# A two-layer encoder trunk on one core: issuing the first weight block, the x blocks and the leading pair's last steps when their engines can begin them, and interleaving the first loads

## The chip, the cores and the metric

The kernel runs on one NeuronCore of a Trainium2 chip. Its engines are TensorE (PE, matrix products into PSUM), VectorE (DVE), ScalarE (ACT), GpSimd (POOL, which here only issues DMAs) and SyncE (SP, which issues DMAs too). Each engine works through its own queue in the order in which the program was written, and waits at an instruction until the semaphores that it names have arrived. The metric is the device time of one execution, in microseconds (us). Before the change it is 1428.33 us, the median of 3 runs (1427.67 to 1429.08).

## The reference

Two layers (`DEPTH = 2`) over 512 tokens of width 1024, all in float32. Cut to what matters here:

```python
for l in range(DEPTH):
    h = rms_norm(x, attn_norm_g[l])
    z = jnp.einsum('bsd,dc->bsc', h, w_in[l])
    qa, ka, va, qb, kb, vb, ga, gb = jnp.split(z, IN_SPLITS, axis=-1)
    ...
    ya = jnp.einsum('bsc,cd->bsd', window_gqa(qa, ka, va, sink_a[l]), w_proj_a[l])
    ...
    yb = jnp.einsum('bsc,cd->bsd', neighbourhood_attn(qb, kb, vb, rel_bias_b[l]), w_proj_b[l])
    mixed = jax.nn.sigmoid(ga) * ya + jax.nn.sigmoid(gb) * yb
    x = x + jnp.einsum('bsd,de->bse', mixed, w_out[l])
    h = rms_norm(x, ffn_norm_g[l])
    u = jax.nn.silu(jnp.einsum('bsd,df->bsf', h, w_gate[l])) * jnp.einsum('bsd,df->bsf', h, w_up[l])
    x = x + jnp.einsum('bsf,fd->bsd', u, w_down[l])
```

`w_in` is 1024 x 4352, the feed-forward width is 2816.

## The kernel before, in words

**Split operands.** Every float32 operand of a product is cut into a high part (a cast to the type that TensorE multiplies, F32R) and a low part (operand minus high part), and a product is three matmuls: high x high, high x low, low x high. A high part is a cast on ACT (`A.copy`), a low part a subtraction on DVE. Where it can be done early, a weight's low part is made by a DMA instead: ACT writes the negated high part, and a DMA of POOL's queue adds the weights to it (`w_low`, `low_by_transfer`).

**The order is written by a planner.** `trunk` runs twice. The first, dry pass keeps a modelled clock per engine (`clock`, `ready`, `cost`) and decides with it when each step is written into the program; the second pass repeats the decisions and emits the instructions. Steps off the main line are generators, called chains: a chain yields a `Need` (tiles that must be ready on an engine, PSUM slots, keys of other steps, and how far that engine's modelled clock may run ahead, `backlog`), and `drive` writes a chain's next step as soon as its `Need` is met at the modelled time of TensorE. A string that the main line yields is a key that must be done before the main line goes on (`force`). Other steps are not asked: `at_pos(t, f)` and `soon(f)` write f at a fixed place in TensorE's modelled order. From the dry pass come also the lifetimes of the SBUF buffers, and `Layout.pack` places them in two arenas (names `arena_72`, float32, and `arena_73`, F32R), so a write can have to wait for the last reader of what lay there before.

**The start.** `x_load(c)` fetches the eight 128-column blocks of x on SP's queue. `first_load(i)` fetches the first projection's weights in four slabs of 512 KB: slab 0 in two halves on ACT's queue, slabs 1 to 3 on POOL's. POOL's queue also carries the small vectors: `consts` (328 KB), the b-branch norm gains (into `vec2`), `positions`, the a-branch norm gains (`gqa`) and the sinks (`snk`). `start(nrm, k)` then prepares block k for the first `token_matmul`: TensorE turns the x block (4 transposes), ACT and DVE make the high and low parts of the weights (`first_parts`) and of x times the norm's gain, and ACT squares. `chain_tables` puts on DVE, among these, the steps of the rotary tables, the first of which read `posi` and `snk`.

**The feed-forward part of a layer.** 2816 hidden columns are one leading pair of 128-column tiles and five quads of 512 columns (`QUADS = 5`). The leading pair is computed in plain form: 48 matmuls of 512 columns for gate, 48 for up (`pair_matmul`), with `evac_g` and `evac_u` taking the results out of PSUM. Each quad is computed by seven block products of a Strassen scheme (`ORDER = (1, 5, 6, 2, 7, 3, 4)`, `m_step`), for gate and then for up: 24 matmuls of 256 columns each. Product m needs the parts of a weight combination (class `Quad`: `high(m)`, `low(m)`) and of an x combination (`chain_x`: blocks b11, b12, b21, b22 of the normalised x, with sums `n1`, `n2`). Products 1, 5 and 2 accumulate in banks of the pool `at`; product 6 goes into a bank of the pool `mm` that ACT first fills with the result of product 1 (`seed`), so product 6 cannot begin before that copy. `seed_c` (DVE) then makes the bank of product 3 out of product 6's. Between the products stand the down-projection steps `("d", ...)`, 6 or 12 matmuls each; the first eight use the leading pair's hidden tiles (`u[0]`, `u[1]`), which `evac_u` multiplies and splits.

**What sets the order around the change.** In each layer the first quad of gate has its steps moved ahead by up to 18 us of modelled time (`early` in `plan_ffn`), `Quad.due` writes `high(m)` 6.5 us before the product's modelled time and `low(m)` 1.8 us later, whatever the engines are doing. `chain_x` writes the cast of a block right behind the instruction that makes it, and `evac_u` writes its five instructions at one go where the pair's last matmul is written.

All instructions are recorded in one helper, so that the profile shows line L309 for nearly all of them; they are told apart by engine, operation and tile. `mm` and `at` are PSUM banks.

## Time and profile before

| | before |
|---|---|
| median of 3 runs | 1428.33 us (1427.67 to 1429.08) |
| profiled execution | 1429.13 us, of which the profile's span is 1426.4 us |
| PE busy | 1393.8 us (98%), 8074 matmuls and transposes |
| DVE, ACT, POOL busy | 935.4, 713.0 and 317.7 us |
| DMA | 208.49 MB, mean 146 GB/s |
| chain that ended last | PE 85%, DVE 10%, ACT 2%, DMA 1% |

Busy time counts from an instruction's start to its end, and neighbours overlap: eight DVE subtractions of 1.22 us that start every 1.14 us keep it busy without a gap. "[5.29 <-ACT mm L309]" behind a row is idle time of that engine just before it, and what ended it.

### The profile page before, as it was taken

What the parts mean: (1) busy time and instruction counts of PE and PEld (TensorE: products, weight loads), DVE (VectorE), ACT (ScalarE), POOL (GpSimd) and SP (SyncE); (2) the same over time, 40 slices, a digit from 0 to 9 for tenths busy, and PEclk for the clock granted to TensorE, in tenths of its full rate; (3) what the DMA queues carried; (4) which work ended last, traced back from release to release, by engine and by line L of the source; (5) the groups of instructions that cost most, each with busy time, mean ns of one, the idle gap of its engine ahead of it and who ended that gap; (6) DMA issues with size and microseconds to landing.
All of it is one profiled execution on the core that took longest, in us unless ns stands there. A gap on an engine that the chain in (4) does not pass through costs nothing.

```text
span 1426.4 us, 20963 instructions
## 1 busy us (share of the span) xinstructions
PE 1393.8 (98%) x8074; PEld 1223.7 (86%) x8074; DVE 935.4 (66%) x1768; ACT 713.0 (50%) x1209; POOL 317.7 (22%) x325
## 2 busy tenths in 40 slices
PE   7999999999989999999999999999998999999998
PEld 5788888888889999999987888888887999999997
DVE  5877788455867566575648869774567657575753
ACT  6476766543653343343545776674445433343441
POOL 4443222310121111101353332223012120111110
PEclk9999999999999999999999999999999999999999
DMA  8877988885486565736798678979557484745545
GB/s 203 171 135 133 165 156 148 158 196 147 91 183 141 119 149 131 180 77 131 148 188 180 125 138 154 172 137 204 146 137 132 121 194 102 177 100 138 129 93 118
DMA packets 197299, 208.49 MB, mean 146 GB/s; under 512 B 25532, under 2 KB 167024, under 8 KB 197200
## 3 DMA queue, kind: packets, MB, share of 16 engines
q0 software_dynamic: 134944, 141.53, 53.6%
q1 hardware_dynamic: 61904, 65.09, 15.7%
q8 instruction: 63, 1.03, 0.3%
q10 hardware_dynamic: 352, 0.54, 0.1%
q14 instruction: 36, 0.29, 0.1%
HBM read 194.55 MB, written 2.10 MB: 138 GB/s over the span
## 4 chain that ended last, share of the span: by engine, by line
PE 85%; DVE 10%; ACT 2%; DMA 1%; issue 1%; POOL 0%; DVEq 0%; ACTq 0%; POOLq 0%
PE mm L309 65%; PE at L309 20%; DVE arena L309 7%; DVE sm L309 3%; ACT arena L309 2%; DMA cst<-in_consts 1%; DMA snk<-in_sink_a 0%; DMA arena<-in_w_in 0%; POOL arena L309 0%; ACT L309 0%; DVE hf L309 0%; ACT mm L309 0%; DVE den L309 0%; ACT sm L309 0%; DVEq L1619 0%
## 5 line engine op out<-in xcount | busy, mean ns | idle before, releaser
L309 PE MATMUL mm<-arena 128*128 128x512 f32 (+1 forms) x5568 | 1126.6, 357 | 15.2 <-ACT mm L309 10.6
L309 PEld LDWEIGHTS mm<-arena 128*128 128x128 f32 x5568 | 906.6, 191 | 147.7 <-ACT mm L309 11.0
L309 ACT CAST arena<-arena 128x1024 fp32r<-128x1024 f32 (+2 forms) x278 | 236.0, 870 | 235.9 <-DVE arena L309 232.6
L309 PE MATMUL at<-arena 128*128 128x256 f32 (+2 forms) x1952 | 301.5, 295 | 1.8 <-DVE arena L309 1.6
L309 DVE TENSOR_TENSOR arena<-arena,arena 128x1024 fp32r<-128x1024 f32 (+2 forms) x268 | 262.2, 993 | 55.5 <-ACT arena L309 55.2
L309 PEld LDWEIGHTS at<-arena 128*128 128x128 f32 x1952 | 265.3, 191 | 20.8 <-DVE arena L309 5.0
L309 ACT ACTIVATE arena<-arena 128x1024 fp32r<-128x1024 f32 (+3 forms) x252 | 207.6, 843 | 122.4 <-DMA arena<-in_w_down 59.0
L309 DVE TENSOR_TENSOR arena<-arena,mm 128x512 f32<-128x512 f32 x144 | 98.9, 687 | 233.3 <-PE mm L309 233.2
L309 POOL DMA_DIRECT2D arena<-in_w_in x163 | 163.1, 1397 | 335.4 <-ACT arena L309 330.6
L309 POOL DMA_DIRECT2D arena<-in_w_down x96 | 99.4, 1233 | 502.4 <-ACT arena L309 316.8
L309 DVE TENSOR_TENSOR arena<-arena 128x1024 f32<-128x1024 f32 (+4 forms) x196 | 158.5, 823 | 2.5
L309 DVE TENSOR_TENSOR arena<-at,arena 128x384 fp32r<-128x384 f32 (+4 forms) x206 | 114.8, 562 | 63.0 <-ACT arena L309 55.5
L309 ACT CAST arena<-at 128x384 fp32r<-128x384 f32 (+2 forms) x164 | 74.6, 458 | 106.9 <-PE at L309 93.0
L309 PE MATMUL at<-cst,arena 128*128 128x128 f32 x504 | 85.7, 276 | 5.2 <-DVE arena L309 4.3
L309 PEld LDWEIGHTS at<-cst,arena 128*128 128x128 f32 x504 | 64.0, 141 | 22.5 <-DVE arena L309 5.8
L309 ACT ACTIVATE arena<-arena,negm 128x256 f32<-128x256 f32 (+1 forms) x128 | 71.5, 560 | 16.8 <-DVE negm L309 16.0
L309 ACT COPY arena<-at 128x512 f32<-128x512 f32 (+1 forms) x68 | 39.5, 582 | 64.0 <-PE at L309 63.6
L309 DVE TENSOR_TENSOR arena<-mm,arena 128x512 f32<-128x512 f32 x72 | 49.3, 687 | 27.2 <-PE mm L309 26.8
L309 DVE CUSTOM_DVE_ANT_0 arena<-at,cst,nsnk 128x256 f32<-128x256 f32 (+1 forms) x64 | 34.5, 546 | 20.0 <-PE at L309 19.8
L309 ACT ACTIVATE arena<-arena,vecT 128x512 fp32r<-128x512 f32 x24 | 17.4, 726 | 54.4 <-DVE arena L309 53.9
L309 DVE CUSTOM_DVE_ANT_0 arena<-at,arena 128x256 f32<-128x256 f32 (+1 forms) x64 | 30.7, 486 | 8.9 <-PE at L309 8.4
L309 POOL DMA_DIRECT2D arena<-in_w_up x8 | 8.2, 1029 | 125.3 <-PE mm L309 77.7
(69 smaller groups left out, 429.7 us busy)
## 6 DMA issues: line engine op xcount, KB each, us to landing
arena<-in_w_in POOLq DMA_DIRECT2D x99, 512.0 KB, 7.2
arena<-in_w_down POOLq DMA_DIRECT2D x80, 512.0 KB, 6.8
arena<-in_w_gate SPq DMA_DIRECT2D x20, 1024.0 KB, 7.2
arena<-in_w_up SPq DMA_DIRECT2D x20, 1024.0 KB, 5.1
arena<-in_w_in POOLq DMA_DIRECT2D x64, 256.0 KB, 6.2
arena<-in_w_proj_a POOLq DMA_DIRECT2D x16, 512.0 KB, 7.2
arena<-in_w_proj_b POOLq DMA_DIRECT2D x16, 512.0 KB, 7.3
arena<-in_w_out SPq DMA_DIRECT2D x16, 512.0 KB, 6.1
```

The lines of the kernel that those rows point to most:

```text
L309: f(*args, **kw)
```

## The change

First quad of gate (class `Quad`, `first`): its steps are no longer written at fixed positions but by a chain, which waits for each product's due position, then writes the sums on DVE, waits until the source is ready for ACT before it writes the cast, and until the cast is ready for DVE before it writes the low part. `chain_x`: every cast now waits in the planner for its source. The leading pair's last steps: `evac_u` only takes the result out of PSUM, and a chain per tile writes the product with the gate, the cast and the low part when their sources are ready; the main line waits for them (keys `u0`, `u1`) before the first down-projection step. The planner's model counts a bank that a matmul adds to as a source. At the start, POOL's queue takes small loads and slabs in turns, and for block 0 the transposes and the cast of x are written ahead of the weights' parts.

```diff
-                start = max([clock[self.key]] + [at_(name_of(x), self.key) for x in aps[1:]])
+                sources = aps if kw.get("start") is False else aps[1:]
+                start = max([clock[self.key]] + [at_(name_of(x), self.key) for x in sources])
...
     def drive(main):
         for u in main:
-            if isinstance(u, str):
+            if isinstance(u, (str, tuple)):
                 force(lambda: u in done)
...
             (self.a11, self.a21), (self.a12, self.a22) = ((t[:, :, :256], t[:, :, 256:]) for t in self.raw)
+            self.s1 = buf([4, 256])
+            if self.first:
+                spawn(self.chain())
 
         def due(self, m, t):
-            at_pos(t - LEAD_PREP, lambda: self.high(m))
+            if self.first:
+                at_pos(t - LEAD_PREP, lambda: done.add((self, m)))
+                return
+            at_pos(t - LEAD_PREP, lambda: (self.sums(m), self.high(m)))
             at_pos(t - LEAD_PREP + 1.8, lambda: self.low(m))
 
-        def high(self, m):
+        def chain(self):
+
+
+            for m in ORDER:
+                yield Need(keys=[(self, m)], backlog=XLOG)
+                self.sums(m)
+                yield Need("act", [self.source(m)])
+                self.high(m)
+                yield Need("dve", [self.parts[m][1]], backlog=XLOG)
+                self.low(m)
+                done.add((self, m, "parts"))
...
+    first_load(0)
     for c in range(KD):
         x_load(c)
-        if c % 2 == 0:
-            first_load(c // 2)
-    GQ.dma_start(cst[:, P:], a["consts"][:, P:])
-    for i, n in enumerate(("q_norm_b", "k_norm_b")):
-        for h in range(2):
-            GQ.dma_start(vec2[2 * i : 2 * i + 2, HD * h : HD * h + HD], a[n])
     posi = cp.tile([P, P], I32, tag="posi", name="posi")
...
+    for i, n in enumerate(("q_norm_b", "k_norm_b")):
+        for h in range(2):
+            GQ.dma_start(vec2[2 * i : 2 * i + 2, HD * h : HD * h + HD], a[n])
+    first_load(1)
     gqa = cp.tile([P, 2, DEPTH, HD], F32, tag="gqa", name="gqa")
...
+    first_load(2)
+    GQ.dma_start(cst[:, P:], a["consts"][:, P:])
+    first_load(3)
...
-        first_parts(k)
         ps = at_bank()
         for b in range(NB):
             T.transpose(ps[:, P * b : P * b + P], xin[k][:, b, :], ident)
+        if k:
+            first_parts(k)
         A.activation(held(nrm.xh[k]), by_columns(ps), AF.Copy, scale=gain(0, k))
+        if not k:
+            first_parts(k)
...
             def high(m, src):
+                yield Need("act", [src], backlog=XLOG)
                 h = buf([4, 256], F32R)
                 A.copy(h, src)
...
-            high(6, n2)
+            yield from high(6, n2)
...
             V.tensor_tensor(t, ps, nrm.rows, ALU.mult)
+            u.append((act(F32R), act(F32R)))
+            spawn(chain_u(j, t))
+
+        def chain_u(j, t):
+            yield Need("dve", [t, gt[j]])
             V.tensor_tensor(gt[j], t, gt[j], ALU.mult)
-            h, lo = act(F32R), act(F32R)
-            split(gt[j], h, lo)
-            u.append((h, lo))
+            yield Need("act", [gt[j]])
+            yield from gsplit(gt[j], *u[j])
+            done.add(f"{key}u{j}")
...
                 yield f"x{l}{m}"
+                if quads[l, q, w].first:
+                    yield (quads[l, q, w], m, "parts")
                 yield from m_step(q, w, m)
...
+                if f0 == 0:
+                    yield f"{key}u0"
+                    yield f"{key}u1"
```

The order of the matmuls on PE and of the loads on SP stays. Three places where the order moves:

ACT, first layer, from the last parts of the quad's weights to the seed of product 6. `CAST ... 128x1024` is a high part of a weight or x block, `ACTIVATE arena_73<-arena_73 128x1024` the negated copy for a low part by transfer, `ACTIVATE arena_72<-arena_72 128x512` the silu of a gate tile, `CAST ... 128x512` the high part of a hidden tile, `COPY mm<-at` the seed. Before:

```order
L309 CAST arena_73<-arena_72 128x1024 x4
L309 ACTIVATE arena_72<-arena_72 128x512 x2
L309 CAST arena_73<-arena_72 128x1024
L309 ACTIVATE arena_73<-arena_73 128x1024
L309 CAST arena_73<-arena_72 128x1024 x3
L309 CAST arena_73<-arena_72 128x512
L309 ACTIVATE arena_73<-arena_73 128x1024
L309 CAST arena_73<-arena_72 128x512
L309 CAST arena_73<-arena_72 128x1024
L309 COPY mm_3506<-at_3474 128x512
```

The same stretch of ACT after the change, to the hidden tiles' casts:

```order
L309 ACTIVATE arena_72<-arena_72 128x512 x2
L309 CAST arena_73<-arena_72 128x1024 x2
L309 ACTIVATE arena_73<-arena_73 128x1024
L309 CAST arena_73<-arena_72 128x1024 x4
L309 ACTIVATE arena_73<-arena_73 128x1024
L309 CAST arena_73<-arena_72 128x1024
L309 ACTIVATE arena_73<-arena_73 128x1024
L309 COPY mm_3501<-at_3464 128x512
L309 CAST arena_73<-arena_72 128x1024
L309 ACTIVATE arena_73<-arena_73 128x512
L309 CAST arena_73<-arena_72 128x1024
L309 COPY arena_72<-at_3497 128x512
L309 CAST arena_73<-arena_72 128x512 x2
```

The two casts of the hidden tiles stood ahead of the seed and now stand behind it; the negated copies of products 3 and 4 now both stand ahead of it.

DVE at the same place, from the copy of the row scales on. `128x1024` rows into arena_73 are low parts, `SCALAR_TENSOR_TENSOR ... vecT 128x512 x4` normalises half of x, `mm_3290`, `mm_3291` are the pair's gate banks, `mm_3401`, `mm_3402` (after the change `mm_3392`, `mm_3393`) its up banks, `mm_3506` (`mm_3501`) the bank of product 6. Before, from the second half of x:

```order
L309 SCALAR_TENSOR_TENSOR arena_72<-arena_72 128x1024
L309 TENSOR_TENSOR arena_72<-mm_3290,arena_72 128x512
L309 TENSOR_TENSOR arena_72<-mm_3291,arena_72 128x512
L309 TENSOR_TENSOR arena_73<-arena_72,arena_73 128x1024 x3
L309 TENSOR_TENSOR arena_72<-arena_72 128x4x256
L309 TENSOR_TENSOR arena_73<-arena_72,arena_73 128x1024
L309 TENSOR_TENSOR arena_72<-arena_72 128x4x256
L309 TENSOR_TENSOR arena_72<-mm_3401,arena_72 128x512
L309 TENSOR_TENSOR arena_72<-arena_72 128x512
L309 TENSOR_TENSOR arena_73<-arena_72,arena_73 128x512
L309 TENSOR_TENSOR arena_72<-mm_3402,arena_72 128x512
L309 TENSOR_TENSOR arena_72<-arena_72 128x512
```

After:

```order
L309 TENSOR_TENSOR arena_73<-arena_72,arena_73 128x1024
L309 SCALAR_TENSOR_TENSOR arena_72<-arena_72,vecT 128x512 x4
L309 SCALAR_TENSOR_TENSOR arena_72<-arena_72 128x1024
L309 TENSOR_TENSOR arena_72<-arena_72 128x4x256
L309 TENSOR_TENSOR arena_72<-mm_3392,arena_72 128x512
L309 TENSOR_TENSOR arena_73<-arena_72,arena_73 128x1024 x3
L309 TENSOR_TENSOR arena_72<-arena_72 128x4x256
L309 TENSOR_TENSOR arena_72<-mm_3393,arena_72 128x512
L309 TENSOR_TENSOR arena_72<-arena_72 128x512
L309 TENSOR_TENSOR arena_73<-arena_72,arena_73 128x1024
L309 TENSOR_TENSOR arena_72<-arena_72 128x512
L309 TENSOR_TENSOR arena_73<-arena_72,arena_73 128x1024
```

The gate evacuations moved ahead of the second half of x, together with one low part, the first up evacuation moved ahead of three low parts, and the low parts of the hidden tiles left this stretch.

POOL's queue at the start. `arena_72<-in_w_in 128x2x512` is a slab of 512 KB:

```order
-L309 DMA arena_72<-in_w_in 128x2x512 x3
-L309 DMA cst<-in_consts 128x656
+L309 DMA posi<-in_positions 4x8x16
 L309 DMA vec_76<-in_q_norm_b 2x64 x2
 L309 DMA vec_76<-in_k_norm_b 2x64 x2
-L309 DMA posi<-in_positions 4x8x16
+L309 DMA arena_72<-in_w_in 128x2x512
 L309 DMA gqa<-in_q_norm_a 128x128
 L309 DMA gqa<-in_k_norm_a 128x128
+L309 DMA arena_72<-in_w_in 128x2x512
+L309 DMA cst<-in_consts 128x656
+L309 DMA arena_72<-in_w_in 128x2x512
 L309 DMA snk<-in_sink_a 128x16
```

The three slabs left the head of the queue and stand between the small loads; the sinks' load stays last.

## Rows read from the trace of the kernel before

**Rows 1.** The page's first part: busy time of each engine, its share of the span, and its instructions.

```profile
PE 1393.8 (98%) x8074; PEld 1223.7 (86%) x8074; DVE 935.4 (66%) x1768; ACT 713.0 (50%) x1209; POOL 317.7 (22%) x325
```

**Rows 2.** Who PE waited for over the whole span: microseconds in total, how often, the longest.

```profile
PE mm L309 <- ACT mm L309: 10.6, 2, 5.3
```

**Rows 3.** The timeline around product 6 of the first layer (start, length, engine, what, how often, idle time before it and what ended it).

```profile
388.71 5.91 PE L309 MATMUL at<-arena 128*128 128x256 f32 x48
...
393.50 0.68 DVE L309 TENSOR_TENSOR arena<-mm,arena 128x512 f32<-128x512 f32 x1
...
394.94 0.62 ACT L309 CAST arena<-arena 128x512 fp32r<-128x512 f32 x1 [0.22 <-DVE arena L309]
...
396.20 0.68 DVE L309 TENSOR_TENSOR arena<-mm,arena 128x512 f32<-128x512 f32 x1
...
397.70 1.56 ACT L309 CAST arena<-arena 128x512 fp32r<-128x512 f32 x2 [1.18 <-DVE arena L309]
...
399.29 0.57 ACT L309 COPY mm<-at 128x512 f32<-128x512 f32 x1
...
399.91 4.66 PE L309 MATMUL mm<-arena 128*128 128x256 f32 x24 [5.29 <-ACT mm L309]
```

**Rows 4.** The timeline of DVE and ACT ahead of it, from the copy of the row scales.

```profile
375.81 0.69 DVE L309 COPY arena<-at 128x512 f32<-128x512 f32 x1
...
376.53 2.74 DVE L309 SCALAR_TENSOR_TENSOR arena<-arena,vecT 128x512 f32<-128x512 f32 x4
...
379.30 1.23 DVE L309 TENSOR_TENSOR arena<-arena 128x1024 f32<-128x1024 f32 x1
380.44 1.22 DVE L309 TENSOR_TENSOR arena<-arena,arena 128x1024 fp32r<-128x1024 f32 x1
380.56 2.00 ACT L309 CAST arena<-arena 128x1024 fp32r<-128x1024 f32 x2 [0.21 <-DVE arena L309]
...
385.49 1.28 DVE L309 TENSOR_TENSOR arena<-mm,arena 128x512 f32<-128x512 f32 x2
...
386.57 1.14 ACT L309 ACTIVATE arena<-arena 128x512 f32<-128x512 f32 x2
386.69 3.48 DVE L309 TENSOR_TENSOR arena<-arena,arena 128x1024 fp32r<-128x1024 f32 x3
...
388.69 1.06 ACT L309 ACTIVATE arena<-arena 128x1024 fp32r<-128x1024 f32 x1
```

**Rows 5.** The chain that ended last, in order of time, at product 6, the product behind it and a later one of the first layer, and at the same two of the second layer (start, length, what, how many instructions).

```profile
399.91 4.66 PE mm L309 x24
404.57 2.88 PE at L309 x24
...
423.12 2.87 PE at L309 x24
...
1097.66 5.49 PE mm L309 x24
1103.15 2.92 PE at L309 x24
```

**Rows 6.** Busy time in four stretches (engines in the order PE, PEld, DVE, ACT, POOL, each with its count; then TensorE's granted clock, the busy share of the DMA engines and GB/s): the start, a wait of PE in the first layer's attention, the wait before product 6, and the stretch behind it.

```profile
4.00:6.00 2.00, 1.34 (x5) 0.89 (x5) 0.19 (x1) 0.26 (x2) 2.00 (x5) 1.00 1.06 368
42.00:44.00 2.00, 1.06 (x7) 1.01 (x8) 1.65 (x7) 2.00 (x5) 0.59 (x1) 1.00 0.88 128
398.00:400.00 2.00, 0.09 (x1) 0.09 (x1) 1.65 (x2) 1.98 (x4) 0.18 (x1) 0.50 0.98 359
404.00:406.00 2.00, 2.00 (x19) 2.00 (x19) 1.32 (x2) 0.00 (x0) 0.40 (x1) 1.00 1.20 171
```

**Rows 7.** PE's timeline at that wait in the attention.

```profile
42.94 0.62 PE L309 MATMUL at<-cst,rstd 128*128 128x128 f32 x4 [1.66 <-DVE rstd L309]
43.32 11.86 PE L309 MATMUL mm<-arena 128*128 128x512 f32 x51
```

**Rows 8.** The timeline of the start: the issue of the three slabs on POOL, the first cast of weights and the cast of x behind it on ACT, PE's first products, the issue of the sinks' load, DVE's first step that reads it, and PE behind that.

```profile
1.37 2.33 POOL L309 DMA_DIRECT2D arena<-in_w_in  x3 [0.33 <-issue]
...
6.87 0.62 ACT L309 CAST arena<-arena 128x512 fp32r<-128x512 f32 x1 [2.60 <-DMA arena<-in_w_in]
7.39 0.68 ACT L309 ACTIVATE arena<-at,vecT 128x512 fp32r<-128x512 f32 x1
...
8.12 2.06 PE L309 MATMUL mm<-arena 128*128 128x512 f32 x3 [2.45 <-ACT arena L309]
...
12.89 0.54 POOL L309 DMA_DIRECT2D snk<-in_sink_a  x1 [0.52 <-DMA cst<-in_consts]
...
18.23 0.17 DVE L309 TENSOR_SCALAR nsnk<-snk 128x16 f32<-128x16 f32 x1 [3.99 <-DMA snk<-in_sink_a]
...
19.05 0.49 PE L309 MATMUL mm<-arena 128*128 128x512 f32 x1 [0.83 <-DVE arena L309]
...
19.72 0.50 PE L309 MATMUL mm<-arena 128*128 128x512 f32 x1 [0.17 <-DVE arena L309]
```

**Rows 9.** The page's last part: loads of `w_down`, KB each, median us from issue to landing; and busy time over a whole gate-and-up quad in the first layer, columns as in rows 6.

```profile
arena<-in_w_down POOLq DMA_DIRECT2D x80, 512.0 KB, 6.8
...
468.00:530.00 62.00, 62.00 (x432) 58.07 (x432) 38.57 (x43) 24.41 (x30) 8.16 (x8) 1.00 0.56 134
```

More of the change, by code (lines that the diff above doesn't have):

```diff
@@ L578, in trunk, with __init__ @@
     class Quad:
-        def __init__(self, w, col, t, by_transfer):
-            self.w, self.col, self.by_transfer = w, col, by_transfer
+        def __init__(self, w, col, t, first):
+            self.w, self.col, self.first = w, col, first
             self.parts = {}
@@ L594, in load, with source, sums @@
             (self.a11, self.a21), (self.a12, self.a22) = ((t[:, :, :256], t[:, :, 256:]) for t in self.raw)
+            self.s1 = buf([4, 256])
+            if self.first:
+                spawn(self.chain())
         def due(self, m, t):
-            at_pos(t - LEAD_PREP, lambda: self.high(m))
+            if self.first:
+                at_pos(t - LEAD_PREP, lambda: done.add((self, m)))
+                return
+            at_pos(t - LEAD_PREP, lambda: (self.sums(m), self.high(m)))
             at_pos(t - LEAD_PREP + 1.8, lambda: self.low(m))
-        def high(self, m):
+        def chain(self):
[7 more added lines that the diff above has]
+                done.add((self, m, "parts"))
+        def source(self, m):
+            return {1: self.a11, 2: self.a12, 3: self.a12, 4: self.a22, 5: self.s1, 6: self.a11, 7: self.a21}[m]
+        def sums(self, m):
             add = lambda o, x, y: V.tensor_tensor(o, x, y, ALU.add)
             if m == 5:
-                self.s1 = buf([4, 256])
                 add(self.s1, self.a21, self.a22)
@@ L609, in high @@
                 add(self.a12, self.a12, self.a11)
-            src = {1: self.a11, 2: self.a12, 3: self.a12, 4: self.a22, 5: None, 6: self.a11, 7: self.a21}[m]
-            src = self.s1 if src is None else src
-            h = buf([4, 256], F32R)
+        def high(self, m):
+            src, h = self.source(m), buf([4, 256], F32R)
             A.copy(h, src)
@@ L618, in low @@
             lo = buf([4, 256], F32R)
-            if self.by_transfer and m not in (1, 2):
+            if self.first and m not in (1, 2):
                 low_by_transfer(lo, src, h)
@@ L1421, in chain_x @@
             yield from normal(0)
-            high(1, b11)
+            yield from high(1, b11)
             V.tensor_tensor(n1, b11, b12, ALU.subtract)
             yield from low(1)
-            high(5, n1)
+            yield from high(5, n1)
             yield from normal(1)
             V.scalar_tensor_tensor(n2, n1, -1.0, b22, ALU.mult, ALU.subtract)
-            high(6, n2)
+            yield from high(6, n2)
             yield from low(5)
             yield from low(6)
-            high(2, b21)
+            yield from high(2, b21)
             yield from low(2)
             V.tensor_tensor(b12, b22, b12, ALU.subtract)
-            high(7, b12)
+            yield from high(7, b12)
             yield from low(7)
-            high(3, b22)
+            yield from high(3, b22)
             yield from low(3)
             V.scalar_tensor_tensor(n1, n2, -1.0, b21, ALU.mult, ALU.subtract)
-            high(4, n1)
+            yield from high(4, n1)
             yield from low(4)
```

## The prediction

> **What bounds the kernel now.** I read the page's busy times first: TensorE (PE) works 1393.8 of 1426.4 us [rows 1], so the change can touch at most the 32.6 us in which PE stands still, and matmuls that run slowly. Who PE waits for comes next [rows 2]: the largest sum, 10.6 us, is two waits of 5.3 us for one ACT instruction that writes a PSUM bank, one wait in each layer. The reader is to see in the timeline [rows 3] which it is. PE finishes products 1 and 5 at 394.62 (388.71 + 5.91) and begins product 6 at 399.91, 5.29 us later. The seed copy that it needs could have run from 391.6 on, when product 1 was done, but it starts at 399.29, because it stands in ACT's queue behind the casts of the two hidden tiles. These wait for DVE (0.22 and 1.18 us), and DVE reaches the pair's up results only at 393.50 and 396.20: a ping-pong between two engines that work in order, with PE's next operand at its end. The third view is the chain that ended last [rows 5]: behind the wait, product 6 takes 4.66 us in the first layer and 5.49 in the second, where such a product takes 2.87. In the wait the granted clock is 0.50, the 1.2 GHz level, and it is back at 1.00 from 404 on [rows 6]. The fourth is the start [rows 8]: PE waits 2.45 us for ACT, and 0.83 and 0.17 us for DVE, which stood 3.99 us waiting for the sinks.
>
> **The wait before product 6, replayed.** I take the new order of DVE and ACT and give each step the distance from its start to the next one's in the trace [rows 4]: 2.77 us for half of x, 1.14 for a DVE step of 1024 columns (379.30 to 380.44), 1.20 for two evacuations (385.49 to 386.69), about 0.65 for one with nothing behind it to wait for, 1.0 for a cast or negated copy on ACT (two casts in 2.00), 0.57 for a silu.
>
> DVE is still busy without a gap from the row scales at 375.81 on, so what counts is where a step stands. First half of x until 379.30, the low part of weight block 2 until 380.44, gate evacuations until 381.64, a difference until 382.78. ACT's silus begin behind the evacuations and end at 382.33; the cast of x block 1, now behind them, ends at 383.33, so DVE waits 0.6 us and has that low part at 384.56. PE needs it at 388.71. Second half of x until 387.33, its sum 388.47, the weight sum for product 3 at 389.61, first up evacuation (its bank is complete 12 matmuls of 0.23 us [rows 7] before 388.71) 390.21, low parts of x blocks 5, 6 and 2 at 391.35, 392.49 and 393.63. PE needs block 5 at 391.6, with 0.25 us to spare, and block 6 at 394.5.
>
> ACT behind 383.33: cast and negated copy for product 7, cast of x block 5 (386.4), a wait for the sum of block 6, casts of x blocks 6 and 2 (390.6), cast and negated copy for product 3 (392.6), the same for product 4 (394.65), and then the seed. PE starts 0.62 us after the seed does (399.29 to 399.91), at 395.27. The wait is 0.65 us in place of 5.29: a gain of 4.64 per layer, **9.3 us in both** (the second layer has the same 5.3 us wait and the same order). Bounds: the whole 5.29, if ACT gains 0.65 us somewhere, and 2.0 us, if ACT is held on the way by a wait as long as the longest of these rows, 2.60 us [rows 8].
>
> **The clock.** If PE waits 0.65 us, product 6 should run at the 2.4 GHz level. The nearest row is the wait of 1.66 us for the row scales [rows 7]: the granted clock around it is 1.00 [rows 6] and the 51 matmuls behind it take 0.23 us each. Then 4.66 + 2.88 become 2 x 2.87 in the first layer (1.80) and 5.49 + 2.92 in the second (2.67): **4.5 us**. Bounds: 0, if a short wait were enough to lower it, and 4.5. [...]
>
> **What is late next.** Product 7 writes the bank that `seed_c` reads. On DVE, behind the second evacuation (395.4), stand a product with the gate, the low parts of x blocks 7 and 3, another such product and a sum, 0.65 + 0.25 (waiting for ACT's cast) + 1.14 + 0.65 + 1.14 + 1.14 = 400.4, then `seed_c`, 0.70. PE is through products 6 and 2 at 395.27 + 5.74 = 401.0 and waits 0.2 us: **+0.4 us** in both layers. The hidden tiles' low parts end at about 403.5; the first down step, at 407, needs them. The first `w_down` low part leaves POOL at about 398 and lands 6.8 us later [rows 9], at 404.7. The second slab is the tightest: its load leaves at about 399, ACT can negate it at 406, the transfer ends near 414, and PE wants it near 415.5, one product and two down steps later. All of that is cover of 1 to 3 us, where 5 more were there before; if it is gone, it costs 1 to 3 us in each layer.
>
> **The start.** Casting x ahead of the weights in block 0 lets that cast run inside ACT's 2.60 us wait: PE's first product comes at the end of the weights' cast, 7.49, plus the usual hop, in place of 8.12, 0.5 us. With the slabs behind the small loads, the first half of slab 0 has the DMA engines, which are at 1.06 of their share at that time [rows 6], more to itself; this can bring a further part of ACT's 2.60 us, of which I count 0 to 1.5. The stall for the sinks costs PE 1.0 us (0.83 + 0.17). The sinks' load stays last on POOL's queue, behind the same bytes, but without waits before it it is issued at 1.37 + 2.33 for three slabs + 8 x 0.54 for eight small loads = 8.0 us rather than at 12.89 [rows 8]. It landed by 18.23, 5.3 us after its issue. So it lands between 13.3 and 18.2, or later, if it has to wait for slabs that now start later. I take **1.5 us** of gain for the start, between +3 (all of this) and -2 (sinks at 21, DVE and PE 2 to 3 us behind). The Trainium skill (DMA: Bandwidth & Descriptors, "Queues, rings and completion order") says that a DMA engine serves in turn the queues that have work. By that the order within POOL's queue only moves shares between it and SP's x blocks, the sinks land no earlier than 18.2, the start gains nothing, and the sum is 13.4; the busy share of 1.06 agrees with it, and its time, 1415, lies inside the forecast's own range.
>
> **Edits that I cost at nothing.** PE's order stays. The planner's new source for accumulating matmuls and the waits on `parts` and `u0` only decide where steps are written. The number of instructions stays within a few.
>
> **Sum.** 9.3 + 4.5 - 0.4 + 1.5 = 14.9 us off the profiled execution of 1429.13: 1414.2. That execution lies 0.8 above the median, so the forecast is 1413.5 us. Nothing downstream should give it back: later, whole quads run with PE busy in every microsecond [rows 9], and DMA at 0.56 of its share.
>
> **Rivals.**
> - *A new wait takes half of it.* Behind the cast of x block 1 the seed still has six casts and three negated copies before it that themselves hang on two DVE sums; block 5 has 0.25 us of slack. If ACT or DVE is 2 us later than in my replay in each layer, PE waits about 2.7 us there; with half of the clock's loss and 1 us for the second down slab, the gain is 14.9 - 4 - 2.2 - 2 = 6.7: about 1421.5. For it: the 0.6 us that DVE already loses to ACT in the replay. Against: DVE's steps are nearly the same number, so the end of its backlog does not move.
> - *The start loses.* Sinks at 21 us: -2 in place of +1.5, about 1417. For it: their place at the end of the queue. Against: the early issue.
> - *The change doesn't do what it says:* the seed moves but product 6 then waits for block 6 or a transferred low part until 399; only the start changes: about 1427. Against: their negated copies stand on ACT ahead of the silus, before 381.
> - *Slower, by buffers.* The dry pass places all buffers anew. If in each of the ten quads one `w_down` slab has to wait for a later reader of its place and lands half its 6.8 us late, PE stands 3.4 us in each: -14.9 + 34 = about 1448. It decides from 1.5 us per quad on. Against: PE has no gap in a quad now [rows 9], and the new program has no more loads of `w_down` that wait for PE than the old one.
>
> **Chances.** Forecast 0.70 (own range 1411 to 1417), half taken 0.15, start loses 0.07, nothing 0.04, slower 0.04. The range to cover 8 in 10 takes in the best bounds (5.29 in both layers and 3 at the start: about 1410.5) and reaches up to the half-taken case: 1410.5 to 1421. A measurement can tell about 0.2%, 2.9 us. Faster by more 0.92 (the first three), within 0.04, slower 0.04.
>
> **What would show it.** Right: the two waits "PE mm <- ACT mm" shrink from 5.3 to below 1.5 us each, the granted clock stays 1.00 there, and product 6 takes 2.87; the seed stands directly behind negated copies on ACT, at about 394.6 less what the start gained; DVE's `nsnk` row has less idle time than 3.99 us. Wrong: PE waits over 2 us at product 5, 6 or 7 or at the first down steps; the second layer gains something else than the first; the time from there to the end of the layer grows; or PE reaches the first layer's gate pair later than before.

## The result and the profile after

The changed kernel takes 1417.37 us (median of 4 runs, 1416.65 to 1418.54), beside 1428.70 for the kernel before on the same chip: ratio 0.9921, 95% interval 0.9904 to 0.9938. It is faster by 11.3 us where 14.9 were forecast, a time of 1413.5. The profiled execution took 1418.54 us with a span of 1416.8. Its first part of the page (answering to [rows 1]) has PE at work for 1.4 us less, of a span that is 9.6 us shorter:

```profile
PE 1392.4 (98%) x8074; PEld 1221.9 (86%) x8074; DVE 934.1 (66%) x1768; ACT 711.6 (50%) x1209; POOL 316.3 (22%) x325
```

So what changed is mostly where PE waits. Its waits over the whole span, two rows (the second answers to [rows 2]):

```profile
PE mm L309 <- DVE arena L309: 4.6, 3, 3.9
...
PE mm L309 <- ACT mm L309: 1.1, 2, 0.6
```

The wait for ACT's bank has shrunk from 10.6 to 1.1 us. A wait for DVE of 3.9 us at its longest stands against it.

PE's timeline of the changed kernel around product 6, in the first and in the second layer (columns as in [rows 3]), with ACT's seed copy ahead of it:

```profile
392.78 5.91 PE L309 MATMUL at<-arena 128*128 128x256 f32 x48
...
397.54 1.06 ACT L309 ACTIVATE arena<-arena 128x1024 fp32r<-128x1024 f32 x1
398.63 0.57 ACT L309 COPY mm<-at 128x512 f32<-128x512 f32 x1
...
399.25 3.14 PE L309 MATMUL mm<-arena 128*128 128x256 f32 x24 [0.56 <-ACT mm L309]
402.22 3.04 PE L309 MATMUL at<-arena 128*128 128x256 f32 x24
...
416.51 3.04 PE L309 MATMUL at<-arena 128*128 128x256 f32 x24
...
1083.96 5.91 PE L309 MATMUL at<-arena 128*128 128x256 f32 x48
1090.43 3.14 PE L309 MATMUL mm<-arena 128*128 128x256 f32 x24 [0.56 <-ACT mm L309]
1093.40 3.04 PE L309 MATMUL at<-arena 128*128 128x256 f32 x24
...
1107.69 3.04 PE L309 MATMUL at<-arena 128*128 128x256 f32 x24
```

The seed stands behind a negated copy, and the wait is 0.56 us where it was 5.29. From the end of the gate pair to the first up product (392.78 to 416.51, 1083.96 to 1107.69) PE takes 23.73 us in both layers. Before, the same stretch ended with these rows in PE's timeline:

```profile
418.69 1.48 PE L309 MATMUL at<-arena 128*128 128x256 f32 x11
...
1086.45 5.91 PE L309 MATMUL at<-arena 128*128 128x256 f32 x48
...
1117.31 2.92 PE L309 MATMUL at<-arena 128*128 128x256 f32 x23
```

That is 418.69 - 388.71 = 29.98 us and 1117.31 - 1086.45 = 30.86 us, so the two stretches gain 6.25 + 7.13 = 13.38 us. But the gate pair of the first layer itself ends at 392.78 in place of 388.71 [rows 3]: the start has lost 4.07 us in this execution, the slowest of the four. The timeline of the start (answering to [rows 8]):

```profile
2.24 1.08 POOL L309 DMA_DIRECT2D vec<-in_q_norm_b  x2
...
6.73 2.18 PE L309 MATMUL mm<-arena 128*128 128x512 f32 x3 [1.28 <-ACT arena L309]
...
8.89 0.56 POOL L309 DMA_DIRECT2D cst<-in_consts  x1 [2.05 <-DMA vec<-in_q_norm_b]
...
10.15 0.56 POOL L309 DMA_DIRECT2D snk<-in_sink_a  x1
...
20.15 0.18 DVE L309 TENSOR_SCALAR nsnk<-snk 128x16 f32<-128x16 f32 x1 [7.37 <-DMA snk<-in_sink_a]
...
20.97 1.46 PE L309 MATMUL mm<-arena 128*128 128x512 f32 x2 [3.95 <-DVE arena L309]
...
22.93 4.80 PE L309 MATMUL mm<-arena 128*128 128x512 f32 x12
27.57 0.60 PE L309 MATMUL at<-cst,arena 128*128 128x128 f32 x4
```

PE's first product starts 1.39 us earlier than before (8.12 [rows 8]). Then DVE stands 7.37 us for the sinks, which land at 20.15 us, and PE 3.95 us behind it. PE goes on 1.92 us later than before (19.05 [rows 8]), and its next 12 matmuls take 4.80 us where the same 12 took 3.00. PE's rows before:

```profile
20.41 3.00 PE L309 MATMUL mm<-arena 128*128 128x512 f32 x12
...
23.26 0.60 PE L309 MATMUL at<-cst,arena 128*128 128x128 f32 x4
```

The windows show why: the granted clock is at 0.50, the 1.2 GHz level, until past 26 us (columns as in [rows 6]; the last row is the stretch of the wait before product 6, where the clock was 0.50 before).

```profile
20.00:22.00 2.00, 1.03 (x2) 0.65 (x3) 1.85 (x4) 0.00 (x0) 0.00 (x0) 0.50 0.78 172
...
26.00:28.00 2.00, 2.00 (x11) 1.60 (x9) 1.83 (x7) 0.61 (x2) 1.60 (x3) 0.80 0.00 0
...
398.00:400.00 2.00, 1.44 (x12) 1.24 (x12) 1.92 (x3) 1.98 (x3) 1.35 (x2) 1.00 1.02 388
```

The balance of the profiled pair at the first up product of the second layer is 1107.69 - 1117.31 = -9.62 us, and the span differs by 9.6: nothing is lost behind the FFN's lead.

### The profile page after: what moved, and what is told of

Same layout as the page of the kernel before. It is cut to its first block, busy times and chain, and to the rows that moved or that the text cites. A ratio compares the mean times of both kernels' runs of the same rounds, so it can differ in the third digit from the quotient of the medians.

```text
span 1416.8 us, 20995 instructions
## 1 busy us (share of the span) xinstructions
PE 1392.4 (98%) x8074; PEld 1221.9 (86%) x8074; DVE 934.1 (66%) x1768; ACT 711.6 (50%) x1209; POOL 316.3 (22%) x325
## 4 chain that ended last, share of the span: by engine, by line
PE 86%; DVE 9%; ACT 3%; DMA 1%; issue 1%; POOL 0%; DVEq 0%; ACTq 0%; POOLq 0%
PE mm L309 66%; PE at L309 20%; DVE arena L309 6%; DVE sm L309 3%; ACT arena L309 2%; DMA snk<-in_sink_a 1%; DMA vec<-in_q_norm_b 0%; ACT L309 0%; DVE hf L309 0%; DVE den L309 0%; ACT mm L309 0%; ACT sm L309 0%; POOL posi L309 0%; POOL arena L309 0%; DVEq L1656 0%
```

## The experiments on the start

The theory: DVE works in order and stands at `nsnk` until the sinks' load, last on POOL's queue, has landed; PE waits behind it and loses its clock. The rival: casting x first in block 0, or slabs that are late in the new order. One mark measures the start in each trace: where the first layer's gate pair ends (388.71 before, 392.78 after).

**The old order of loads, everything else changed.**

```
-    first_load(0)
     for c in range(KD):
         x_load(c)
+        if c % 2 == 0:
+            first_load(c // 2)
+    GQ.dma_start(cst[:, P:], a["consts"][:, P:])
...
-    first_load(1)
...
-    first_load(2)
-    GQ.dma_start(cst[:, P:], a["consts"][:, P:])
-    first_load(3)
```

> The changed kernel with the loads in the old order (slabs between x blocks, small loads behind all slabs); casts of block 0 and the FFN edits stay. Theory (the new load order makes the sinks land 2 us later, DVE stands there in order, PE waits 3.95 us and runs slowly after): sinks land by 18.2 us, the granted clock is not at 0.50 from 20 to 26 us, the gate pair of layer 1 ends at 388 +- 0.7 us in place of 392.8, and the time is about 1413. Rival (the 4 us come from casting x ahead of the weights in block 0, or from the placing of buffers): the gate pair still ends near 392.8 and the time stays 1417.

Measured: 1414.84 us (1414.45 to 1416.45), ratio 0.9904 (0.9891 to 0.9918); gate pair at 388.45.

```profile
7.90 2.19 PE L309 MATMUL mm<-arena 128*128 128x512 f32 x3 [2.10 <-ACT arena L309]
...
18.26 0.17 DVE L309 TENSOR_SCALAR nsnk<-snk 128x16 f32<-128x16 f32 x1 [3.98 <-DMA snk<-in_sink_a]
...
19.08 0.50 PE L309 MATMUL mm<-arena 128*128 128x512 f32 x1 [1.99 <-DVE arena L309]
```

The theory's mark is met, and the rival falls: block 0's casts lose nothing. They win nothing either: PE is ahead, waits 1.99 us in place of 0.83, and goes on at 19.08, where it went on at 19.05 before. Whatever is won ahead of the sinks is swallowed by them. The time is 1.8 us above the 1413 expected. DVE still stands there for 3.98 us, and the last run of this section, without that stand, takes 1412.29 us.

**The new order of loads alone, on the kernel before** (the same edit the other way round).

> The kernel before with the new order of loads alone. Theory (load order): sinks land near 20 us, PE waits some 4 us for DVE there, the gate pair of layer 1 ends near 393 in place of 388.7, and the time is 1432 to 1433. Rival (the loads are harmless, block 0's casts or the buffers lose the time): gate pair within 1 us of 388.7, time 1428 to 1429.

Measured: 1430.03 us (1428.62 to 1432.18), ratio 1.001 (1.0001 to 1.0019); gate pair at 390.12. Neither expectation is met.

```profile
9.46 0.56 POOL L309 DMA_DIRECT2D snk<-in_sink_a  x1
...
18.29 0.17 DVE L309 TENSOR_SCALAR nsnk<-snk 128x16 f32<-128x16 f32 x1 [5.36 <-DMA snk<-in_sink_a]
...
19.11 0.50 PE L309 MATMUL mm<-arena 128*128 128x512 f32 x1 [3.07 <-DVE arena L309]
...
20.46 4.58 PE L309 MATMUL mm<-arena 128*128 128x512 f32 x12
```

Here the sinks landed at 18.29, as early as before, though issued 3.4 us earlier. The loss is the clock alone: PE was further ahead, waited 3.07 us and ran the 12 matmuls in 4.58 us in place of 3.00. So the load order costs in two ways: a longer wait with the low clock behind it, in all five profiles with this order and `nsnk` in its place, and a later landing in some executions (18.29 to 20.15 us in these five). The changed kernel's profile has the latest of these landings. In three later profiles (the first three runs of the next section), whose start has the same steps in the same order, the gate pair ends at 390.64, 392.00 and 392.04 us: the start loses 1.9 to 4.1 us, by the execution.

**`nsnk` later, behind the tables of sines; the new order of loads stays.**

```
-        yield Need("dve", [posi, snk, gqa])
+        yield Need("dve", [posi, gqa])
         V.tensor_copy(vec2[64:68], posi[64:68])
-        V.tensor_scalar(nsnk, snk, -1.0, None, ALU.mult)
...
+        yield Need("dve", [snk])
+        V.tensor_scalar(nsnk, snk, -1.0, None, ALU.mult)
         done.add("trig")
```

> The changed kernel with its new load order, but the instruction that needs the sinks (nsnk, used only by the attention heads) moved behind the tables of sines, some 20 instructions of DVE later. Theory A (what costs is DVE waiting in order for the sinks, which land at 20.15 us): DVE does not stand there, PE's wait of 3.95 us and the stretch at 0.50 go, the gate pair of layer 1 ends at 387 to 388.7, the time is 1411 to 1413. Theory B (all loads are late in this order, the slabs too, and DVE would wait for the next one): a wait of 2 us or more turns up at a slab or at x within the next blocks, the gate pair ends at 391 or later, time 1415 to 1417.

Measured: 1413.26 us (1412.44 to 1413.80), ratio 0.9891 (0.9877 to 0.9904); gate pair at 387.97.

```profile
16.44 0.60 PE L309 MATMUL at<-cst,arena 128*128 128x128 f32 x4
...
24.22 0.73 PE L309 MATMUL mm<-arena 128*128 128x512 f32 x2 [1.34 <-ACT arena L309]
```

Theory A holds: one DVE instruction moved gives the start 4.81 us back. B holds in small: PE is 5.8 us ahead at 16.44 (it began the same transposes at 22.23) and gives a part back at the next late thing, a cast on ACT behind a slab that came late.

**The small loads ahead of the slabs.**

```
+    for i, n in enumerate(("q_norm_a", "k_norm_a")):
+        GQ.dma_start(gqa[:, i], a[n].rearrange("l d -> (l d)").unsqueeze(0).to_broadcast([P, DEPTH * HD]))
...
+    GQ.dma_start(snk, a["sink_a"].rearrange("l h -> (l h)").unsqueeze(0).to_broadcast([P, DEPTH * 8]))
     first_load(1)
-    for i, n in enumerate(("q_norm_a", "k_norm_a")):
-        GQ.dma_start(gqa[:, i], a[n].rearrange("l d -> (l d)").unsqueeze(0).to_broadcast([P, DEPTH * HD]))
     first_load(2)
     GQ.dma_start(cst[:, P:], a["consts"][:, P:])
     first_load(3)
...
-    GQ.dma_start(snk, a["sink_a"].rearrange("l h -> (l h)").unsqueeze(0).to_broadcast([P, DEPTH * 8]))
```

> The changed kernel with all small loads but the masks (positions, norms, query and key gains, sinks) ahead of the slabs on POOL's queue. Theory A (the sinks are late only because they are queued behind three slabs and the masks): they land before 13 us, DVE does not stand for them, gate pair of layer 1 ends at 387 to 388.7, time 1411 to 1413. Theory B (the transfers are short of DMA engines, whatever comes last is late): the slabs, now issued 1.6 us later, land late and PE or ACT waits for them for 2 us or more, gate pair at 390 to 392, time 1414 to 1417.

Measured: 1413.28 us (1412.67 to 1413.78), ratio 0.9891 (0.9878 to 0.9905); gate pair at 387.50.

```profile
12.91 0.18 DVE L309 TENSOR_SCALAR nsnk<-snk 128x16 f32<-128x16 f32 x1 [0.34 <-DMA snk<-in_sink_a]
```

ACT waits 3.05 us for the second slab, but PE, after its first product, waits nowhere in the start for more than 0.54 us. Both ways of removing the stand are worth the same, which is what the theory wants.

**The gains and sinks behind all slabs, `nsnk` late.**

```
     first_load(1)
+    first_load(2)
+    GQ.dma_start(cst[:, P:], a["consts"][:, P:])
+    first_load(3)
...
-    first_load(2)
-    GQ.dma_start(cst[:, P:], a["consts"][:, P:])
-    first_load(3)
...
-        yield Need("dve", [posi, snk, gqa])
+        yield Need("dve", [posi])
...
-        V.tensor_scalar(nsnk, snk, -1.0, None, ALU.mult)
...
+        yield Need("dve", [snk, gqa])
+        V.tensor_scalar(nsnk, snk, -1.0, None, ALU.mult)
         done.add("trig")
```

The second block of lines stood between the loads of `gqa` and of `snk`.

> The changed kernel with the query and key gains and the sinks loaded behind all slabs, and nsnk computed behind the tables of sines: the slabs are issued some 1.1 us earlier than with the small loads first, and nothing waits for the late ones. If the slabs are what bounds the start once DVE doesn't stand for the sinks: ACT's waits for slabs of 0.95 to 3.1 us shrink by about 1 us each, the gate pair of layer 1 ends at 386.5 to 387.5 us, time 1411.5 to 1413. If all bytes of the start have to land anyway by about 21 us: the same 387.5 to 388, time 1413 to 1414.

Measured: 1412.71 us (1412.53 to 1413.04), ratio 0.9889 (0.9874 to 0.9904); gate pair at 387.05. ACT's longest wait for a slab falls from some 3.1 us (in each of the last two runs) to 1.39, and of that 0.5 to 0.9 us arrive at the gate pair.

**The old order of loads and `nsnk` late** (the first edit of this section and the third together).

> The changed kernel with the loads in the old order (as in the run with the old loads, 1414.84 us, where DVE still stood 3.98 us for the sinks) and nsnk computed behind the tables of sines. What is open: whether the new order of loads is worth anything once DVE doesn't stand for the sinks (with the new order and late nsnk: 1413.26 us, gate pair at 387.97). If the stand for the sinks was all there was to lose or gain: gate pair of layer 1 at 387.5 to 388.2 us, time 1413 to 1414. If the new order itself helps (slabs spread among the small loads): PE reaches block 2 later, gate pair at 388.4 or later, time 1414.5 or more. If the old order is better by itself: gate pair below 387.3, time below 1412.7.

Measured: 1412.29 us (1411.94 to 1413.52), ratio 0.9891 (0.9875 to 0.9908); gate pair at 385.93, the earliest of all.

```profile
385.93 5.91 PE L309 MATMUL at<-arena 128*128 128x256 f32 x48
```

PE works without a wait from 9.66 to 27.0 us: the slabs, issued first, are there. So the trace shows the old order reaching the gate pair 2.04 us earlier than the new one, once nothing stands for the sinks. But it is the fastest of its four executions, and that of the new order (1413.80 us) the slowest; the medians differ by 0.97 us and the times overlap. Beside the first run of this section, the stand for the sinks costs 388.45 - 385.93 = 2.5 us in the old order; in the new one it cost 4.8 us in the profiled execution.

## The experiments on the FFN's lead

Four edits were made there at once. The planner's new source for accumulating matmuls was not run alone. With that line as before, all five engines get the same steps in the same order; only places of buffers, and the waits on them, differ. What this placing does to the time is not shown. The others are told apart by the stretch from the gate pair's end to the first up product (29.98 and 30.86 us before, 23.73 and 23.73 after).

**The hidden tiles at once, as before.**

```
-            u.append((act(F32R), act(F32R)))
-            spawn(chain_u(j, t))
-
-        def chain_u(j, t):
-            yield Need("dve", [t, gt[j]])
             V.tensor_tensor(gt[j], t, gt[j], ALU.mult)
-            yield Need("act", [gt[j]])
-            yield from gsplit(gt[j], *u[j])
+            h, lo = act(F32R), act(F32R)
+            split(gt[j], h, lo)
+            u.append((h, lo))
```

> The changed kernel with the hidden tiles made at once as before (evacuation, product with the gate, cast and low part in one go, so both casts stand on ACT ahead of the seed); everything else stays changed. The place to read is the stretch from the end of the gate pair to the first up product, 29.98 and 30.86 us before, 23.73 us in both layers after. Theory (the ping-pong over the hidden tiles is what held the seed): DVE reaches the second evacuation about 5.5 us behind the gate pair's end and ACT the seed about 7.3 us behind it, so PE waits 2 us or more in each layer, stretch at least 25.2 us, time 1420 to 1427. Rival (the quad's chain and the order of the casts of x carry the gain, the hidden casts are small): the wait stays below 1 us, the stretch below 24.5 us, time 1417 to 1418.

Measured: 1422.00 us (1421.36 to 1422.80), ratio 0.9954 (0.9939 to 0.9969); stretches 416.89 - 390.64 = 26.25 and 1110.50 - 1084.46 = 26.04 us.

```profile
390.64 3.15 PE L309 MATMUL at<-arena 128*128 128x256 f32 x25
395.35 3.02 PE L309 MATMUL at<-arena 128*128 128x256 f32 x23 [1.55 <-DVE arena L309]
399.11 3.14 PE L309 MATMUL mm<-arena 128*128 128x256 f32 x24 [0.74 <-ACT mm L309]
```

The theory's size is met, at another place: DVE makes the hidden tile's low part ahead of that of x block 5, so PE waits 1.55 us at product 5 already, and 0.74 is left for the seed.

**The quad's parts at fixed positions, as before.**

```
             self.s1 = buf([4, 256])
-            if self.first:
-                spawn(self.chain())
...
-            if self.first:
-                at_pos(t - LEAD_PREP, lambda: done.add((self, m)))
-                return
...
-                if quads[l, q, w].first:
-                    yield (quads[l, q, w], m, "parts")
```

> The changed kernel with the first quad's weight parts made at fixed positions as before, without the chain and its waits. Theory (moving the hidden tiles alone is enough): wait for the seed below 1 us, stretch from the gate pair's end to the first up product 23.7 to 24.5 us, time 1417 to 1418. Rival (a cast of weights whose DVE sum isn't ready holds ACT, and with it the seed): PE waits 2 us or more before product 6 or 7, stretch 25.5 us or more, time 1420 to 1427.

Measured: 1416.03 us (1415.41 to 1416.74), ratio 0.9912 (0.9897 to 0.9927); stretches 415.05 - 392.00 = 23.05 and 1105.60 - 1082.54 = 23.06 us, better than the changed kernel.

```profile
392.00 5.91 PE L309 MATMUL at<-arena 128*128 128x256 f32 x48
...
397.17 0.57 ACT L309 COPY mm<-at 128x512 f32<-128x512 f32 x1
397.65 1.07 ACT L309 ACTIVATE arena<-arena 128x1024 fp32r<-128x1024 f32 x1
...
397.79 3.14 PE L309 MATMUL mm<-arena 128*128 128x256 f32 x24
```

The seed now stands ahead of a negated copy for a later product, not behind it (397.54 and 398.63 after), and PE doesn't wait at all. Beside the two other edits the chain costs 0.68 us per layer, by one copy that nobody needed yet.

**The casts of x without their wait.**

```
             def high(m, src):
-                yield Need("act", [src], backlog=XLOG)
+                yield from ()
```

> The changed kernel in which the casts of the x blocks are issued as soon as their turn comes, as before, not when ACT could begin them. Theory (moving the hidden tiles alone is enough): stretch 23.7 to 24.5 us, time 1417 to 1418. Rival (the casts then stand on ACT ahead of steps that could run, and what is late is an operand, not the seed): the seed itself is early, but PE waits 2 us or more at product 5, 6, 7 or 3 for DVE or ACT, stretch 25.5 us or more, time 1420 to 1427.

Measured: 1436.68 us (1436.15 to 1438.02), ratio 1.0055 (1.0038 to 1.0072), slower than before; stretches 425.79 - 392.04 = 33.75 and 1126.53 - 1093.41 = 33.12 us.

```profile
394.68 2.00 ACT L309 CAST arena<-arena 128x1024 fp32r<-128x1024 f32 x2 [2.69 <-DVE arena L309]
399.36 1.04 ACT L309 CAST arena<-arena 128x1024 fp32r<-128x1024 f32 x1 [2.67 <-DVE arena L309]
400.42 0.57 ACT L309 COPY mm<-at 128x512 f32<-128x512 f32 x1
...
401.05 5.49 PE L309 MATMUL mm<-arena 128*128 128x256 f32 x24 [3.09 <-ACT mm L309]
...
421.66 4.29 PE L309 MATMUL mm<-arena 128*128 128x256 f32 x28 [2.03 <-DMA arena<-arena]
```

ACT stands 2.69 and 2.67 us in front of casts whose sums DVE hasn't made, and the seed behind them. The quad's negated copies come later still, and their transfers land late. The rival was right that the loss is over 2 us, but the seed wasn't early, and the time lies beyond its 1427.

I then held that the waits of the casts of x are the larger half, and took each of the two edits alone, on the start with the gains last (1412.71 us, which leaves the sinks out of the comparison).

**Only the waits of x** (the first two edits of this section together: hidden tiles and quad as before).

> On the start of the run with the gains and sinks loaded last: of the FFN edits only the waits of the casts of x stay, the hidden tiles are made at once and the quad's parts at fixed positions as before. Theory (the casts of x standing on ACT before their sums are ready are the larger half; undone alone they lost 19 us, the hidden tiles 4.7): stretch from the gate pair's end to the first up product 25 to 26.5 us, time 1412.7 + 2 to 5 = 1414.7 to 1417.7. Rival (the hidden tiles decide, and undoing the x waits was so dear only together with the quad's chain): the old wait for the seed is back, stretch 28.5 to 31 us, time 1422 to 1427.

Measured: 1429.66 us (1427.96 to 1430.43), ratio 1.0008 (0.9999 to 1.0018). PE's waits over the whole span, the two rows that matter:

```profile
PE mm L309 <- ACT mm L309: 10.7, 2, 5.3
...
PE mm L309 <- DMA arena<-in_w_down: 2.8, 2, 1.4
```

My theory falls: with the x waits alone the whole old wait is back (10.6 before [rows 2]), and 2.8 us for down slabs beside it; the stretches are 417.55 - 386.64 = 30.91 and 1117.45 - 1086.67 = 30.78 us. The hidden tiles' casts again stand on ACT right ahead of the seed. The rival's stretch (28.5 to 31) is met, its time (1422 to 1427) is exceeded.

**Only the hidden tiles** (the second and the third edit together: casts of x and quad as before).

> On the same start: of the FFN edits only the hidden tiles' late casts stay; the casts of x are issued when their turn comes and the quad's parts at fixed positions, as before. Theory (the x waits are the larger half): the casts of x stand on ACT with their sums not ready, the seed behind them, stretch 27 us or more, time 1419 or more. Rival (the hidden tiles decide): stretch 23.05 to 24.5 us, time 1411.3 to 1414.3.

Measured: 1422.16 us (1421.71 to 1422.79), ratio 0.9955 (0.9940 to 0.9970); stretches 414.80 - 386.57 = 28.23 and 28.23 us (1110.76 - 1082.53).

```profile
395.44 0.57 ACT L309 COPY mm<-at 128x512 f32<-128x512 f32 x1
...
396.06 4.59 PE L309 MATMUL mm<-arena 128*128 128x256 f32 x24 [3.58 <-ACT mm L309]
```

Alone it shortens the wait from 5.3 to 3.58 us, not enough to keep the clock (4.59 us for the product). So neither edit is a half of its own: with the quad by position, they bring alone nothing and 1.75 + 2.63 = 4.4 us in the stretches, together 30.86 + 29.98 - 23.05 - 23.06 = 14.7. Each removes one of two things that stand between the seed and its turn on ACT, and with the quad by position the clock is kept only when both are gone. What the quad's chain is worth depends on its company: added to the x waits alone it shortens the stretches from 30.91 and 30.78 to 26.25 and 26.04 us, with the clock kept (first run of this section); added to the hidden tiles alone it lengthens them from 28.23 to 33.75 and 33.12; added to both it costs 0.68. The chain alone was not run.

**Both repairs: gains and sinks last, quad by position** (two edits shown above, together).

> Both repairs together: the start of the run with the gains and sinks loaded last (1412.71 us), and the first quad's weight parts at fixed positions as before (there PE had no wait before product 6, and 23.05 us from the gate pair's end to the first up product in place of 23.73). If the two places are independent: gate pair of layer 1 ends near 387.0 us, stretch 23.05 us in both layers, time 1412.7 - 2 x 0.68 = 1411.35 us, within 0.7. If the start only moved the wait (what the quad's chain costs hung on the late start): stretch back at 23.7 and time 1412.7.

Measured: 1411.78 us (1410.91 to 1411.95), ratio 0.9881 (0.9866 to 0.9895); gate pair at 387.12, stretches 23.05 and 23.06 us. The two places are independent, and this is the fastest kernel run, 5.6 us faster than the changed one. The old order of loads with late `nsnk` and the quad by position wasn't tried; from 1412.29 - 2 x 0.68 I estimate 1410.9 us.

## Why the prediction was right, and where it was wrong

- **The wait before product 6: right.** Forecast 0.65 us per layer, measured 0.56 in both. The seed stands 398.63 - 392.78 = 5.85 us behind the gate pair's end, where the replay had 394.65 - 388.71 = 5.94. All else in the term rests on that replay of two engines in their new order, and it held to 0.1 us.
- **The clock: right.** Product 6 takes its 2.97 us start to start in both layers, and the granted clock did not fall. From the wait's end to the first up product it is 17.26 us in both, before 18.78 and 19.65: 3.9 us of gain, where 4.5 - 0.4 were in the sum.
- **Product 7 and the down slabs: smaller than put in.** PE waits for neither. ACT does wait 3.3, 3.1 and 5.2 us for down slabs, but not on PE's path; the cover held.
- **The start: wrong, and this is the step that failed.** The term was 1.5 us won and came out as 4.07 us lost in the profiled execution, outside its own bounds (3 won, 2 lost); the sign of being wrong that the prediction named, PE later at the first layer's gate pair, came true. Three things in it failed. The issue of the sinks' load was put at 8.0 us "without waits before it"; POOL waited 2.05 us, and it came at 10.15. The landing was put between 13.3 us, 5.3 us behind the issue as before, and 18.2, "or later"; it came at 20.15, 10.0 us behind the issue. In this order an earlier issue was no earlier landing (issued at 9.46 it landed at 18.29, where 12.89 gave 18.23). And the clock was left out: a longer wait of PE in the same place, paid once more at the low clock, was 2.4 of the 4.31 us (the transposes at 23.26 before, 27.57 after, less 1.92 for the sinks). The sum had only asked what the casts win, not that the stand for the sinks swallows it. The rival "the start loses" gave sinks at 21 us and 1417; that is what happened, and its chance of 0.07 was too small. By the Trainium skill (DMA: Bandwidth & Descriptors, "Queues, rings and completion order"), where a DMA engine serves in turn the queues that have work, the prediction reckoned with no landing before 18.2. All five profiles with this order agree (18.29 to 20.15), which does not yet show that this rule is the cause.
- **Edits costed at nothing.** The planner's source moves no step, and was not run alone. Wrong for the quad's chain, which beside the other edits costs 0.68 us per layer by the place of one negated copy.
- **The sum.** Without the start it was 13.4; with the start as measured, 13.4 - 4.07 = 9.3 in the profiled pair, and 9.6 were measured. So 1417.37 lies within 1410.5 to 1421, but above the forecast's own 1411 to 1417, and the range held because it reached up to the half-taken case, not because the start was understood. With the stand for the sinks removed the kernel takes 1413.26 or 1413.28 us, where 1413.5 were forecast; that this is so close is in part luck, since the forecast holds 1.5 us won at the start, and these two traces show 388.71 - 387.97 = 0.74 and 388.71 - 387.50 = 1.21.

## What to carry to other kernels

Ahead of an engine that works in order, ask of each instruction whether what it waits for is there, not only whether it is cheap: one DVE step of 0.18 us, first needed 63 us later (by an attention step at 83.7 us), cost 2.5 to 4.8 us in these profiles because it stood first. Work won ahead of a fixed landing is lost at it, and if the wait grows, the clock makes it worse. Where several edits free one instruction, undo them one at a time and also try each alone: here the parts did not add up, and one of them was better left out beside the two others.

## What the runs showed that was not expected

**POOL's loads wait for earlier loads of other tiles.** In each trace of the start a load on POOL waits for the landing of the load eight before it. In the changed kernel the masks' load, the tenth, waited for the second (2.05 us). With the small loads first, the ninth waited 0.32 us for the first, and the tenth for the second:

```profile
8.08 0.72 POOL L309 DMA_DIRECT2D arena<-in_w_in  x1 [1.12 <-DMA vec<-in_q_norm_b]
```

So a small load that lands late holds the issue of a slab eight places behind. Four such small loads stand in a row here. Why the issue waits is not shown.

**Small loads land late.** The list of DMA issues in the changed kernel, in the first 30 us (KB each, median us from issue to landing):

```profile
vec<-in_q_norm_b POOLq DMA_DIRECT2D x2, 0.5 KB, 6.3
...
snk<-in_sink_a POOLq DMA_DIRECT2D x1, 8.0 KB, 10.0
```

Half a kilobyte takes 6.3 us beside the slabs, 8 KB takes 10.0; the 8 KB of `in_attn_norm_g`, issued at 0.74 us ahead of all slabs, take 1.8.

**PE's clock behind a wait.** Waits of 0.56, 0.74, 1.55 and 1.99 us left the matmuls behind them at the 2.4 GHz level (24 in 3.14 us, 23 in 3.02, 12 in 3.01); behind waits of 2.65, 3.07, 3.58, 3.95 and 5.33 us they ran wholly or in part at the 1.2 GHz level (12 in 3.87, 4.58 and 4.80 us, 24 in 4.59 and 5.49 us). But the length of the wait alone does not settle it. In the run with the casts of x without their wait, PE waits 2.03 us in each layer for a transferred low part: behind the first of these waits (421.66 us, above) the granted clock stays at 1.00, behind the second, which ends at 1112.17 us, it falls to 0.50 (1114 to 1116 us):

```profile
1112.17 9.10 PE L309 MATMUL mm<-arena 128*128 128x256 f32 x54 [2.03 <-DMA arena<-arena]
```

And at the start the granted clock is no guide: before 14 us it reads 1.00 in the changed kernel, while 12 matmuls from 9.41 us on take 4.74 us.
